# Rotation tables of a two-layer attention trunk: one pass per group for all blocks, and loads that repeat the rows

## The chip, the cores and the metric

The kernel runs on one core of a Trainium2 chip. The metric is the device time of one execution in microseconds (us). The engines of the core are named as the profile names them: PE (TensorE, matrix products), DVE (VectorE), ACT (ScalarE), POOL (GpSimd) and SP (SyncE, which here issues every DMA).

## What is computed

The reference is a trunk of two layers over a sequence of 2048 frames with 1024 channels. Each layer projects its input, runs four groups of attention heads side by side, gates them, projects the result back and applies a layer norm. Two of the four groups rotate queries and keys by position:

```
def _rope(x, positions):
    d = x.shape[-1]
    inv_freq = ROPE_THETA ** (-jnp.arange(0, d, 2) / d)
    ang = positions[..., None] * inv_freq
    cos, sin = jnp.cos(ang)[:, :, None, :], jnp.sin(ang)[:, :, None, :]
    x1, x2 = jnp.split(x, 2, axis=-1)
    return jnp.concatenate([x1 * cos - x2 * sin, x2 * cos + x1 * sin], axis=-1)

def _layer(x, ...):
    proj = x @ w_in                       # 14 parts
    ya = banded attention with relative bias     (A: own chunk + 8 before)
    yb = latent attention; q_rope and k_rope of 32 channels are rotated   (B)
    yc = banded attention; q and k of 64 channels are rotated             (C: own chunk + 2 before)
    ym = attention to 256 memory tokens                                   (M)
    y = concat(ya*silu(ag), yb*silu(bg), yc*silu(cg), ym*silu(mg)) @ w_out
    return layer_norm(alpha * x + y)
```

The angles depend on the positions alone, not on the layer.

## The kernel before

The sequence is cut into four blocks of 512 frames (`BT`), and everything is held with channels on the 128 partitions and frames along the row. Products keep fp32 accuracy by splitting each operand into a high and a low part (`xh`, `xl`, `whi`, `wlo`) and adding three products.

For each layer the program lists units: for each block one unit of C for each pair of heads, M, A, C, M, A (24 units), then for each pair of heads and block a unit of B (`unit_b`, 8 units). A unit has a fill (projections, rotation, row maxima: small steps) and attention banks. `drive` puts the fill of the next unit between the banks of the present one. `later(dt, f)` puts work some modelled time behind. The framework then orders the instructions of each engine by its own estimate; each engine executes its queue in order, and all DMAs go out on SP's queue in order.

Rotation tables: group 0 (C) has 32 frequencies, group 1 (B) has 16. A table has 128 rows: for a block, row p holds the cosine (or the sine with a sign) of position x frequency p mod 32 (or mod 16). `trig(b, gs)` loads the 512 positions of block b, repeated over 128 partitions (L281), converts them (L283, DVE), and for each group runs 11 more DVE instructions and two sines on ACT, whose function tables are switched to the sine and back to the exponential, and stores the tables in DRAM (L300, L301). It is called in layer 0 alone: group 0 of block 0 in `mem_kv` at the start, group 1 of block 0 in the first M unit, and both groups of block b + 1 in the last A unit of block b.

The tables come back through two buffers `cts` (cosine, sine; one of each, 256 KB), at three places: L731 and L732 in each unit of C (group 0, 16 times in all), L827 and L828 in `latent` with k = 0 (group 1, 8 times), and L968 and L969 in `unit_b` (group 1, 16 times). In layer norm (`phase3`) `cts` holds the gain.

In `unit_b`, `qrdone` multiplies the projected rotary queries by the tables and, some modelled 3 us later, issues four loads that put them into the query tiles (L1035, L1036, named Y<-xh and Y<-xl). The products for the row maxima (`mx`) read them. The `tmp` tiles (5 buffers of 512 columns) hold the positions and the angles as well as loaded inputs and other short-lived values.

Of the kernel before, what the change touches and what calls it, by code (L numbers as in the profile page):

```python
# [149 lines left out]
def hybrid(ctx, tc, x, mem, positions, w_in, rel_bias, q_norm, w_uq, kv_norm, w_ukv,  # L150
# [17 lines left out]
    def act(out, a, fn, **kw):  # L168
        ck.use("act", 0.17 + 0.00083 * cols(out), out, a)
        return nc.scalar.activation(out, a, fn, **kw)  # L170
# [35 lines left out]
    def tmp(name, dt=F32):  # L206
        return sb.tile([128, BT], dt, name=name, tag="tmp", bufs=5)

    def rowcast(src, off, n):
        return bass.AP(tensor=src.tensor, offset=src.offset + off, ap=[[0, 128], [1, n]])  # L210
# [54 lines left out]
            return [o, o + 1024, o + 2048]  # L265
        return [4096 + 1024 * (b - 1), 4096 + 3072 + 1024 * (b - 1), 4096 + 6144 + 1536 * (b - 1)]

    cosT, sinT, memkv = {}, {}, {}
    h_src = [x[0, t * 128:(t + 1) * 128, :] for t in range(S // 128)]

    def setup_rows():
# [4 lines left out]
            act(rr[0:32, 0:c1 - c0], rf[0:32, 0:c1 - c0], AF.Copy)  # L276
            dma(f32(rowt)[:, c0:c1], f32(rr)[0:32, 0:c1 - c0])

    def trig(b, gs=(0, 1)):
        pi = tmp("pi", I32)  # L280
        dma(pi, rowcast(positions, b * BT, BT))  # L281
        pf = tmp("pf")
        nc.vector.tensor_copy(pf, pi)  # L283
        for g in gs:
            ang, kk = tmp("ang"), tmp("kk")
            nc.vector.tensor_scalar(ang, pf, rc[:, g:g + 1], None, op0=OP.mult)
            nc.vector.tensor_scalar(kk, ang, float(np.float32(1.0 / TWO_PI)), ROUND, op0=OP.mult, op1=OP.add)
            nc.vector.tensor_scalar(kk, kk, -ROUND, None, op0=OP.add)
            for pc in (PC1, PC2, PC3):
                stt(ang, kk, -pc, ang, op0=OP.mult, op1=OP.add)  # L290
            nc.vector.tensor_scalar(ang, ang, 3.1415925, -3.1415925, op0=OP.min, op1=OP.max)
            nc.vector.tensor_scalar(kk, ang, -1.0, None, op0=OP.mult)
            tt(kk, kk, ang, op=OP.max)
            nc.vector.tensor_scalar(kk, kk, -1.0, float(np.float32(math.pi / 2)), op0=OP.mult, op1=OP.add)
            act(ang, ang, AF.Sin)
            act(kk, kk, AF.Sin)
            nc.vector.tensor_scalar(ang, ang, rc[:, 2 + g:3 + g], None, op0=OP.mult)
            cosT[g, b] = dram.tile([128, BT], F32, name=f"cos{g}{b}")
            sinT[g, b] = dram.tile([128, BT], F32, name=f"sin{g}{b}")
            dma(cosT[g, b], kk)  # L300
            dma(sinT[g, b], ang)  # L301


    wsrc = []
# [420 lines left out]
    def unit_c(l, b, p, D):  # L725
        qq = [next_q(), next_q()]
        st = {}
        fill = []

        def tabl():  # L730
            dma(cts[0], cosT[0, b])  # L731
            dma(cts[1], sinT[0, b])  # L732
            if p == 0 and b:
                for k in range(2):
                    dma(f32(Kc[k][0])[:, 0:128], f32(Kc[k][0])[:, BT:BT + 128])
                    dma(f32(Kc[k][1])[0:64, 0:128], f32(Kc[k][1])[0:64, BT:BT + 128])
                dma(f32(Vc)[:, 0], f32(Vc)[:, 4])
        fill.append((0.0, tabl))

        def kdone(r):  # L740
            for k in range(2):
                split_k(r[k], Kc[k][0][:, 128:], Kc[k][1][:, 128:])

        def qdone(r):
            for i in range(2):
                split_q(r[i], 0.125, *qq[i])
            st["q"] = True

        def gdone(pg):
            st["ge"] = gate_tiles(pg)  # L750

        def maxes(i):
            h = 2 * p + i
            k1 = Kc[p][0]
            q1, q2 = qq[i]

            def one(t):
                def f():
                    if t == 0:
                        ck.until(lambda: "q" in st)  # L760
                        st["mc", i] = mcol(4)
                    mc = st["mc", i]
                    if t % 2 == 0:
                        st["m"] = bank("mx", "mx")
                    lo = 0 if b or t else 128
                    o = 256 * (t % 2)
                    mt = st["m"][:, o + lo:o + 256]
                    ck.tick(mmc(mt, q1[:, 128 * t:128 * t + 128], k1[:, 128 * t + lo:128 * t + 256], True, True))
                    ttr(mt, cmask[:, lo:256], mc[:, t:t + 1], snk[:, 4 * l + h:4 * l + h + 1])
                    if t == 3:  # L770
                        max_row(mc, q2, 64, st, i)
                return f
            return [(0.107, one(t)) for t in range(4)]

        pq = project((l, b, 10 + 2 * p), lambda pp: rope(pp, qdone))
        pg = project((l, b, 11 + 2 * p), gdone)
        if p == 0:
            fill += project((l, b, 8), lambda pp: rope(pp, kdone))
            fill += pq
            fill += project((l, b, 9), lambda pp: put_v(pp, Vc, 1, 4))  # L780
            fill += pg
            late = maxes(0) + maxes(1)
        else:
            fill += pq
            lat = []
            for k in range(3):
                lat += project((l, b, 18 + k), lambda pp, k=k: latent(l, b, k, pp, D))
            fill += lat + [(0.0, lambda: latent_fin(l, b, D))]
            fill += pg
            late = maxes(0) + maxes(1)  # L790
        if p == 0:
            fill = fill[:-4] + mix(fill[-4:], late)
        else:
            fill = fill[:-8] + mix(fill[-8:], late)
        banks = []
        for i in range(2):
            h = 2 * p + i
            q1, q2 = qq[i]
            k1, k2 = Kc[p]
            hd = mk_head(st, i, 64 * p, lambda: st["ge"], D["gT"][4 + p, b], srow[p])  # L800

            def sink(q2=q2, h=h):
                bias = snk[64:65, 4 * l + h:4 * l + h + 1]
                act(es[0:1], f32(q2)[64:65], AF.Exp, bias=bias)
                ef = tmp("ef")
                act(ef[0:1], f32(q2)[64:65], AF.Exp, bias=bias)
                tt(es[32:33], ef[0:1], f32(es)[0:1], op=OP.subtract)

            def sg(t, q0, qe, col):
                ks = slice(128 * t, 128 * t + 128)  # L810
                vh, vl = vst(Vc, t, p)
                return seg(q0, qe, col, d64_ops(k1[:, ks], k2[0:73, ks], q1, q2, q0, qe), vh, vl)
            bl = head_banks(hd, [[sg(1, 0, 256, 0), sg(2, 128, 384, 256)],
                                 [sg(3, 256, 512, 0), sg(4, 384, 512, 256)] + ([sg(0, 0, 128, 384)] if b else [])])
            bl[0]["sink"] = sink
            banks += bl
        return fill, banks

    def latent(l, b, k, p, D):
# [4 lines left out]
        if n == 64:  # L824
            nc.gpsimd.memset(sf[64:128], 0.0)
        if k == 0:
            dma(cts[0], cosT[1, b])  # L827
            dma(cts[1], sinT[1, b])  # L828
            D["sums", b] = sb.tile([128, 3, 4], F32, name="sums", bufs=2)
        later(0.8, lambda: dma(D["lat"][k, b][:n], cf[:n]))  # L830
        if k == 1:
# [117 lines left out]
    def unit_b(l, b, p, D):  # L949
# [13 lines left out]
        def loads():  # L963
            for k in (0, 2):
                dma(f32(lat[k]), f32(D["lathl"][k, b]).rearrange("p (s c) -> p s c", s=2))
            for z in range(2):
                dma(f32(lat[1])[64 * z:64 * z + 64, 0], f32(D["lathl"][1, b])[:, BT * z:BT * z + BT])
            dma(cts[0], cosT[1, b])  # L968
            dma(cts[1], sinT[1, b])  # L969
            for i in range(2):  # L970
                kh, kl = kpart(i, b)
                dma(f32(kh)[96:101], f32(rowt)[26:31, 0:BT])
                dma(f32(kh)[64:96], f32(D["kr"][0, b]))
                dma(f32(kl)[64:96], f32(D["kr"][1, b]))
            if (b, p) in ((0, 0), (1, 0)):
                for q in qq:
                    dma(f32(q[0])[97:101, :], f32(rowt)[4:8, 0:BT])
            v = vpart(b)
            nc.gpsimd.memset(f32(v)[:, :, 1, :], 1.0)
            nc.gpsimd.memset(f32(v)[:, :, 4, :], 0.0)  # L980
            for i in range(2):
                g = sb.tile([128, BT], F32, name="gm", tag="gate", bufs=6)
                st["ge", i] = g
            dma(st["ge", 0], D["gB"][p, b])
            later(2.5, lambda: act(st["ge", 1], st["ge", 0], AF.Exp, scale=-1.0))
# [207 lines left out]
    def mem_kv(kq):  # L1193
# [2 lines left out]
        wload(0)  # L1196
        f()
        dma(rc, rope_c)
        trig(0, (0,))
        wload(1)  # L1200
        run_fill(st)
        wsplit(0)
# [215 lines left out]
    for l in range(L):  # L1418
# [13 lines left out]
        else:  # L1432
            kq()
            load_mem(l)
        units = []
        for b in range(NB):
            us = [unit_c(l, b, 0, D), None, None, None, None, None]
            us[1] = unit_m(l, b, 0, D)
# [9 lines left out]
            if b == 0:  # L1448
                us[2] = ([(0.0, lambda: (ka(), bias_tables(l, D)))] + us[2][0], us[2][1])
            if l == 0 and b == 0:  # L1450
                us[1][0].insert(0, (0.0, lambda: trig(0, (1,))))
            if l == 0 and b + 1 < NB:
                us[5][0].insert(2, (0.0, lambda b=b: trig(b + 1)))
            units += us
        for p in range(2):
            for b in range(NB):
# [62 lines left out]
```

## Time and profile before

| | |
|---|---|
| time, 3 runs | 2660.25 us median, 2650.18 to 2664.6 |
| the profiled execution's own time | 2660.33 us |
| its span, first to last instruction | 2658.5 us |
| mean granted TensorE clock | 0.984 |
| busy | PE 2517.0 us (95%), DVE 1864.5 (70%), ACT 1258.8 (47%), POOL 1071.2 (40%) |
| DMA | 350.90 MB in 176443 packets, mean 132 GB/s |

Busy shares are averages over the span; an idle stretch of PE is what costs time. The granted clock is the share of full speed at which PE was allowed to run.

### The profile page before, as it was taken

The numbers are of one execution on the slowest core, as the hardware profiler recorded it, in microseconds if no ns is written. First come the engines' busy times: TensorE is split into PE (matmuls) and PEld (weight loads), VectorE is DVE, ScalarE is ACT, GpSimd is POOL, SyncE is SP. The second block draws the span as 40 slices with busy tenths as digits, with TensorE's granted clock in tenths as the row PEclk, the third lists the DMA queues.
The fourth block names the chain that finished last, engine by engine and source line by source line (L and its number), as shares of the span: only waits on it lengthen the run. The fifth ranks groups of instructions, "written<-read, shape, count | busy, mean of one in ns | idle before, by whom it ended". The sixth has DMA issues, their size and how long they took to land. (4 is left out here: it accounts for less than half of the span.)

```text
span 2658.5 us, 36518 instructions
## 1 busy us (share of the span) xinstructions
PE 2517.0 (95%) x12312; PEld 2072.1 (78%) x12312; DVE 1864.5 (70%) x3309; ACT 1258.8 (47%) x2251; POOL 1071.2 (40%) x835
## 2 busy tenths in 40 slices
PE   7999999999999899989999999999999999999998
PEld 6777877877888777768877778788788777777786
DVE  4667767658666877878766566567567577588786
ACT  4544455545544566650025444454454555666200
POOL 3343434343443344353343434434434433435343
PEclk9999999999999999999999999999999999999999
DMA  6555345345345423244445443443443453232432
GB/s 208 159 159 168 107 140 158 110 132 166 106 129 169 150 78 98 71 152 145 140 136 160 150 145 127 126 138 118 143 139 115 144 168 104 68 114 78 150 124 87
DMA packets 176443, 350.90 MB, mean 132 GB/s; under 512 B 25689, under 2 KB 48945, under 8 KB 176257
## 3 DMA queue, kind: packets, MB, share of 16 engines
q1 hardware_dynamic: 176256, 348.58, 41.9%
q8 instruction: 98, 1.61, 0.3%
q14 instruction: 89, 0.72, 0.1%
HBM read 247.43 MB, written 68.02 MB: 119 GB/s over the span
## 5 line engine op out<-in xcount | busy, mean ns | idle before, releaser
L182 POOL TENSOR_TENSOR wlo<-raw,whi 128x1024 fp32r<-128x1024 f32 (+1 forms) x192 | 459.5, 2393 | 660.5 <-ACT whi L170 622.9
L350 PE MATMUL pp<-xh,whi 128*128 128x512 f32 x1472 | 591.8, 402 | 7.0 <-DVE Y L174 4.4
L350 PE MATMUL pp<-xl,whi 128*128 128x512 f32 x1472 | 583.4, 396 | 4.6 <-DVE xl L174 4.5
L350 PE MATMUL pp<-xh,wlo 128*128 128x512 f32 x1472 | 580.1, 394 | 0.0
L170 ACT ACTIVATE ph<-sc 128x512 fp32r<-128x512 f32 (+2 forms) x560 | 324.1, 579 | 359.5 <-PE sc L350 350.5
L350 PE MATMUL sc<-Y 96*128 96x512 f32 (+16 forms) x1840 | 454.8, 350 | 11.8 <-DMA Y<-mr 5.8
L174 DVE TENSOR_TENSOR pl<-p,ph 128x512 fp32r<-128x512 f32 (+2 forms) x389 | 319.6, 823 | 186.9 <-ACT p L170 182.2
L350 PE MATMUL pv<-ph,Y 128*128 128x512 f32 (+3 forms) x1520 | 396.7, 341 | 9.3 <-DVE e L178 5.4
L350 PEld LDWEIGHTS sc<-Y 96*128 96x128 f32 (+6 forms) x1840 | 315.9, 193 | 56.0 <-DMA Y<-mr 5.7
L170 ACT ACTIVATE whi<-raw 128x1024 fp32r<-128x1024 f32 x192 | 203.6, 1060 | 325.2 <-PE pp L350 119.2
L182 POOL TENSOR_TENSOR pl<-p,ph 128x512 fp32r<-128x512 f32 (+1 forms) x171 | 221.1, 1293 | 329.0 <-ACT p L170 243.5
L350 PEld LDWEIGHTS pp<-xh,whi 128*128 128x128 f32 x1472 | 279.6, 190 | 63.1 <-issue 5.1
L350 PEld LDWEIGHTS pp<-xh,wlo 128*128 128x128 f32 x1472 | 278.7, 189 | 59.2
L170 ACT ACTIVATE p<-sc 128x512 f32<-128x512 f32 (+2 forms) x560 | 322.4, 576 | 0.8 <-DVE pl L174 0.4
L350 PEld LDWEIGHTS pp<-xl,whi 128*128 128x128 f32 x1472 | 279.9, 190 | 49.8 <-DVE xl L174 6.7
L350 PEld LDWEIGHTS pv<-ph,Y 128*128 128x128 f32 x1520 | 271.3, 191 | 50.1 <-issue 5.9
L350 PE MATMUL pv<-pl,Y 128*128 128x512 f32 (+3 forms) x760 | 265.0, 349 | 34.3 <-DVE pl L174 22.4
L350 PE MATMUL mx<-Y 128*128 128x256 f32 (+6 forms) x800 | 249.6, 339 | 23.7 <-DVE Y L178 10.9
L495 DVE CUSTOM_DVE_ANT_0 mx<-mx,bts 128x128 f32<-128x128 f32 (+3 forms) x352 | 171.9, 495 | 73.3 <-PE mx L350 66.7
L350 PEld LDWEIGHTS mx<-Y 128*128 128x128 f32 (+1 forms) x800 | 148.4, 191 | 77.8 <-DVE Y L178 17.7
L182 POOL TENSOR_TENSOR g<-g,e 128x128 f32<-128x128 f32 x192 | 116.6, 616 | 206.3 <-DVE e L190 191.6
L350 PEld LDWEIGHTS pv<-pl,Y 128*128 128x128 f32 x760 | 145.4, 191 | 65.6 <-DVE pl L174 33.5
(235 smaller groups left out, 3594.4 us busy)
## 6 DMA issues: line engine op xcount, KB each, us to landing
raw<-in_w_in_dram SPq DMA_DIRECT2D x184, 512.0 KB
Y<-Y SPq DMA_DIRECT2D x144, 128.0 KB
gr<-gT SPq DMA_DIRECT2D x64, 256.0 KB
gT<-g SPq DMA_DIRECT2D x48, 256.0 KB
cts<-sin SPq DMA_DIRECT2D x40, 256.0 KB
cts<-cos SPq DMA_DIRECT2D x40, 256.0 KB
xt<-in_xT_dram SPq DMA_DIRECT2D x32, 256.0 KB
raw<-in_w_out_dram SPq DMA_DIRECT2D x16, 512.0 KB
```

What stands on the lines that cost most here:

```text
L170: return nc.scalar.activation(out, a, fn, **kw)
L174: return nc.vector.tensor_tensor(out, a, b, **kw)
L182: return nc.gpsimd.tensor_tensor(out, a, b, **kw)
L350: mm(o, lhs, rhs, start=start, stop=stop)
L495: nc.vector.tensor_tensor_reduce(m, m, table, op0=OP.add, op1=OP.max, scale=1.0, scalar=floor, accum_out=acc)
```

## The change

One pass per group makes the tables of all four blocks: block b has its positions on partitions 32b to 32b + 31 (four loads of 32 partitions, `trig_pos`), so that row 32b + i is block b's frequency i. The pass is a list of 13 steps (`trig`): group 0 runs at the start as before, group 1 is mixed step by step into the fill of the first M unit. The passes for blocks 1 to 3 are gone. Each group stores three parts in one DRAM tile: cosine, and sine and its negative in the order that the group needs; the sign is no longer a multiplication by a constant column.

The loads (`tload`) now repeat rows: the cosine load reads the 32 rows of a block four times; the sine table is put together from pieces that alternate between sine and negative sine, two loads of 64 partitions for group 0, four of 32 partitions for group 1.

```
-    def trig(b, gs=(0, 1)):
+    def trig_pos():
         pi = tmp("pi", I32)
-        dma(pi, rowcast(positions, b * BT, BT))
-        pf = tmp("pf")
-        nc.vector.tensor_copy(pf, pi)
-        for g in gs:
-            ang, kk = tmp("ang"), tmp("kk")
...
-            act(ang, ang, AF.Sin)
-            act(kk, kk, AF.Sin)
-            nc.vector.tensor_scalar(ang, ang, rc[:, 2 + g:3 + g], None, op0=OP.mult)
-            cosT[g, b] = dram.tile([128, BT], F32, name=f"cos{g}{b}")
-            sinT[g, b] = dram.tile([128, BT], F32, name=f"sin{g}{b}")
-            dma(cosT[g, b], kk)
-            dma(sinT[g, b], ang)
+        for b in range(NB):
+            dma(pi[32 * b:32 * b + 32], bass.AP(tensor=positions.tensor, offset=positions.offset + b * BT,
+                                                ap=[[0, 32], [1, BT]]))
+        return pi
+
+    def trig(g, pi):
...
+        def start():
+            st["a"], st["k"] = tmp("ang"), tmp("kk")
+            nc.vector.tensor_copy(st["k"], pi)
+        def sine():
+            act(st["a"], st["a"], AF.Sin)
+            act(st["k"], st["k"], AF.Sin)
+            t = trigt[g] = dram.tile([3 * 128, BT], F32, name=f"trig{g}")
+            dma(t[0:128], st["k"])
+            dma(t[128 * (1 + g):128 * (2 + g)], st["a"])
+        def neg():
+            st["n"] = tmp("nsin")
+            nc.vector.tensor_scalar(st["n"], st["a"], -1.0, None, op0=OP.mult)
+            dma(trigt[g][128 * (2 - g):128 * (3 - g)], st["n"])
...
+
+    def tload(g, b):
+        t = trigt[g][32 * b:32 * b + 1, 0:1]
+        n = 32 >> g
+        dma(cts[0], bass.AP(tensor=t.tensor, offset=t.offset, ap=[[0, 4], [BT, 32], [1, BT]]))
+        for i in range(2 + 2 * g):
+            r = slice(2 * n * i, 2 * n * i + 2 * n)
+            dma(cts[1][r], bass.AP(tensor=t.tensor, offset=t.offset + 128 * BT,
+                                   ap=[[(128 + g * n) * BT, 2], [BT, n], [1, BT]]))
...
         def tabl():
-            dma(cts[0], cosT[0, b])
-            dma(cts[1], sinT[0, b])
+            tload(0, b)
...
-            dma(cts[0], cosT[1, b])
-            dma(cts[1], sinT[1, b])
+            tload(1, b)
...
-            dma(cts[0], cosT[1, b])
-            dma(cts[1], sinT[1, b])
+            tload(1, b)
...
-        trig(0, (0,))
+        for f_ in trig(0, trig_pos()):
+            f_()
...
             if l == 0 and b == 0:
-                us[1][0].insert(0, (0.0, lambda: trig(0, (1,))))
-            if l == 0 and b + 1 < NB:
-                us[5][0].insert(2, (0.0, lambda b=b: trig(b + 1)))
+                us[1] = (mix(us[1][0], [(0.0, lambda: tg.extend(trig(1, trig_pos())))]
+                             + [(0.0, lambda: tg.pop(0)())] * 13),) + us[1][1:]
```

## Rows read from the trace of the kernel before

**Rows 1.** Head of the page and busy time by engine.
```profile
span 2658.5 us, 36518 instructions
...
PE 2517.0 (95%) x12312; PEld 2072.1 (78%) x12312; DVE 1864.5 (70%) x3309; ACT 1258.8 (47%) x2251; POOL 1071.2 (40%) x835
```
**Rows 2.** Windows, L827 of block 0 to 3, layers 0 and 1 (columns in its heading).
```profile
core 0: us, PE busy (x) PEld busy (x) DVE busy (x) ACT busy (x) POOL busy (x), PEclk, DMA share, GB/s
147.50:758.10 610.60, 582.67 (x2920) 483.49 (x2919) 427.94 (x785) 307.91 (x520) 243.17 (x166) 0.98 0.44 137
1450.00:2049.10 599.10, 585.11 (x3017) 485.04 (x3016) 381.78 (x716) 292.51 (x502) 240.44 (x166) 1.00 0.42 133
```
**Rows 3.** Groups of PE, 1450 to 2049.1 us: busy, mean ns, idle before.
```profile
L393 PE MATMUL px<-identr,xt 128*128 128x128 f32 x96 | 14.1, 273 | 0.7 <-DMA xt<-h 0.7
```
**Rows 4.** Timeline of PE: start, duration, instruction, [idle before, and what ended it].
```profile
216.16 1.19 PE L350 MATMUL pv<-ph,Y 128*128 128x512 f32 x2 [5.36 <-DVE e L178]
...
599.79 0.80 PE L350 MATMUL mx<-Y 128*128 128x256 f32 x2 [3.72 <-DVE Y L178]
```
**Rows 5.** Windows round the first and the third pass, columns as in rows 2.
```profile
205.00:225.00 20.00, 14.64 (x66) 11.94 (x65) 19.66 (x34) 11.71 (x17) 4.15 (x4) 0.83 0.47 151
...
590.00:640.00 50.00, 43.69 (x204) 36.61 (x203) 38.51 (x64) 23.95 (x38) 16.54 (x11) 0.90 0.50 156
```
**Rows 6.** List of DMA issues, 84 groups: first, two others, last.
```profile
raw<-in_w_in_dram SPq DMA_DIRECT2D x184, 512.0 KB
...
cts<-sin SPq DMA_DIRECT2D x40, 256.0 KB
...
Y<-mr SPq DMA_DIRECT2D x128, 2.0 KB
...
rowt<-rr SPq DMA_DIRECT2D x1, 16.0 KB
```
**Rows 7.** Packets and SP's queue on the page: packets, MB, share of 16 engines.
```profile
DMA packets 176443, 350.90 MB, mean 132 GB/s; under 512 B 25689, under 2 KB 48945, under 8 KB 176257
...
q1 hardware_dynamic: 176256, 348.58, 41.9%
```
**Rows 8.** Timelines of SP and PE in a unit_b of layer 0.
```profile
909.94 0.33 SPq L968 DMA_DIRECT2D cts<-cos  x1
910.66 0.33 SPq L969 DMA_DIRECT2D cts<-sin  x1
...
912.67 0.58 SPq L1035 DMA_DIRECT2D Y<-xh  x1
...
916.45 0.62 PE L350 MATMUL mx<-Y 96*128 96x512 f32 x2
```
**Rows 9.** Timelines of SP and PE in a unit_b of layer 1.
```profile
2324.23 0.34 SPq L968 DMA_DIRECT2D cts<-cos  x1
...
2325.43 0.39 SPq L969 DMA_DIRECT2D cts<-sin  x1
2326.99 1.21 SPq L1035 DMA_DIRECT2D Y<-xh  x2
...
2329.08 0.47 PE L350 MATMUL mx<-Y 96*128 96x512 f32 x1 [0.22 <-DMA Y<-xh]
```
**Rows 10.** Timelines of SP and DVE at the start of layer 1.
```profile
1369.00 0.34 SPq L732 DMA_DIRECT2D cts<-sin  x1
...
1371.85 0.69 DVE L174 TENSOR_TENSOR u<-pp,cts 128x512 f32<-128x512 f32 x1 [1.18 <-DMA cts<-sin]
```
**Rows 11.** Windows over the B units of both layers, columns as in rows 2.
```profile
860.00:1180.00 320.00, 294.16 (x1393) 237.99 (x1391) 254.36 (x456) 210.49 (x411) 141.12 (x119) 0.98 0.34 106
2150.00:2410.00 260.00, 243.59 (x1171) 198.43 (x1170) 200.41 (x395) 164.40 (x326) 101.16 (x92) 0.97 0.35 105
```
**Rows 12.** Waits of PE: us in all, times, longest.
```profile
PE mx L350 <- DMA Y<-xh: 0.5, 2, 0.2
```

More of the change, by code (lines that the diff above doesn't have):

```diff
@@ L266, in mla_kv @@
         return [4096 + 1024 * (b - 1), 4096 + 3072 + 1024 * (b - 1), 4096 + 6144 + 1536 * (b - 1)]
-    cosT, sinT, memkv = {}, {}, {}
+    trigt, memkv = {}, {}
     h_src = [x[0, t * 128:(t + 1) * 128, :] for t in range(S // 128)]
@@ L277, in setup_rows @@
             dma(f32(rowt)[:, c0:c1], f32(rr)[0:32, 0:c1 - c0])
-    def trig(b, gs=(0, 1)):
+    def trig_pos():
         pi = tmp("pi", I32)
-        dma(pi, rowcast(positions, b * BT, BT))
-        pf = tmp("pf")
-        nc.vector.tensor_copy(pf, pi)
-        for g in gs:
-            ang, kk = tmp("ang"), tmp("kk")
[L286 to L294, printed above, removed]
-            act(ang, ang, AF.Sin)
-            act(kk, kk, AF.Sin)
-            nc.vector.tensor_scalar(ang, ang, rc[:, 2 + g:3 + g], None, op0=OP.mult)
-            cosT[g, b] = dram.tile([128, BT], F32, name=f"cos{g}{b}")
-            sinT[g, b] = dram.tile([128, BT], F32, name=f"sin{g}{b}")
-            dma(cosT[g, b], kk)
-            dma(sinT[g, b], ang)
@@ new lines, in trig_pos, with sc, red @@
+        for b in range(NB):
[3 more added lines that the diff above has]
+    def trig(g, pi):
+        st = {}
+        def sc(o, i, *c, **k):
+            return lambda: nc.vector.tensor_scalar(st[o], st[i], *c, **k)
+        def red(pc):
+            return lambda: stt(st["a"], st["k"], -pc, st["a"], op0=OP.mult, op1=OP.add)
+        def start():
[11 more added lines that the diff above has]
+            dma(trigt[g][128 * (2 - g):128 * (3 - g)], st["n"])
+        return [start,
+                sc("a", "k", rc[:, g:g + 1], None, op0=OP.mult),
+                sc("k", "a", float(np.float32(1.0 / TWO_PI)), ROUND, op0=OP.mult, op1=OP.add),
+                sc("k", "k", -ROUND, None, op0=OP.add)] + [red(pc) for pc in (PC1, PC2, PC3)] + [
+                sc("a", "a", 3.1415925, -3.1415925, op0=OP.min, op1=OP.max),
+                sc("k", "a", -1.0, None, op0=OP.mult),
+                lambda: tt(st["k"], st["k"], st["a"], op=OP.max),
+                sc("k", "k", -1.0, float(np.float32(math.pi / 2)), op0=OP.mult, op1=OP.add),
+                sine, neg]
@@ L1435, in hybrid @@
         units = []
+        tg = []
         for b in range(NB):
```

## Prediction

> **What bounds the kernel now.** The head of the page comes first: TensorE (PE) is busy for 95% of a span of 2658.5 us [rows 1], so whatever leaves PE alone is worth nothing, and whatever stops PE counts in full. I then looked for a stretch that does the same work with and without the table passes. Layer 1 makes no tables, so I cut both layers at the same instruction, the first table load of the q latent (L827), from block 0 to block 3, and asked for busy times by stretch [rows 2]. Layer 0 needs 610.6 us, layer 1 599.1 us. The counts show that the comparison is clean: DVE has 785 - 716 = 69 more instructions in layer 0 and ACT 520 - 502 = 18 more, which is what the passes for blocks 1 to 3 issue there (6 groups of 11 and 3 casts on DVE; 12 sines and 6 loads of ACT's tables). PE has 97 more in layer 1, 96 of them the transposes by which layer 1 gets its input, 14.1 us busy [rows 3]. Next I asked PE's timeline for the waits inside those passes. PE stands still for 5.36 us for DVE e, and 3.72 us for DVE Y; three more such gaps (2.25, 3.29, 2.52 us) lie at 388, 397 and 627 us [rows 4]: DVE executes in order, and the table arithmetic, or its wait for the positions, stands ahead of what PE needs. After each gap the granted clock falls: 0.83 of full speed over 20 us round the first pass, 0.90 over 50 us round the third, against 1.00 in layer 1's whole stretch [rows 2, 5]. Last, I read the DMA part of the page, the list of DMA issues and SP's timeline where the tables are loaded, since that is where the change adds work.
>
> **What the passes give back.** Blocks 1 to 3 lose their passes: 69 DVE instructions, 427.94 - 381.78 = 46.2 us of DVE, and 15.4 us of ACT [rows 2]. Most of that runs under PE and is worth nothing. What PE gets back I bound from both sides. Below: 610.6 - 599.1 = 11.5 us, as if the transposes cost nothing. Above: 11.5 + 14.1 = 25.6 us, as if each transpose held PE for its whole duration. A second way: PE idles 27.9 us in layer 0 and 14.0 in layer 1, 13.9 more, and 2% of the clock over 610.6 us is another 12.2; together 26.1, partly the same time twice, since idle time at a low clock counts in both. I take 20.
>
> **What stays.** The start still has one pass of about the same 12 DVE instructions and 2 sines; its positions come by four loads instead of one, three more issues of some 0.35 us on SP ahead of the weight and input loads, but one temporary buffer fewer is held. The pass for the second group is the same work, now spread over one unit. Its start instruction has to wait for the last of four position loads, and the wait stands at the head of DVE's queue with the q splits and row maxima behind it, for which PE waits. For both I take nothing, with -4 to +4 as ends. Ten table stores go away (16 to 6).
>
> **The loads that repeat rows.** This is the added work. 80 loads of 256 KB become 168: per table pair one of 256 KB, and two of 128 KB (first group, 16 times) or four of 64 KB (second group, 24 times). Three things count.
>
> First, SP: 88 more issues at about 0.35 us [rows 8, 9], 31 us of a queue that in most places waits for others soon after. Alone it makes what stands behind a load late by 0.4 to 1.1 us.
>
> Second, the engines that carry them. The bytes are the same, but not the shape: the DRAM side of the cosine load begins with a count of 4 (four copies), and that of each sine piece with a count of 2. How many of the 16 DMA engines a load of few rows uses can be counted. The list has 1,695 issues in 84 groups [rows 6]. If every issue ended with one small packet on each of 16 engines, that would be 27,120 packets; with the 896 that carry rows of 4, 16 or 32 bytes (gn, rc and snk) 28,016 packets below 512 B. The page counts 25,689 [rows 7], 2,327 fewer. 212 issues in the list move 4, 5, 8 or 9 rows (128 of them are the Y<-mr loads of 4 rows [rows 6]); if each uses as many engines as it has rows, 2,328 packets are missing. So a load of few rows runs on few engines. In all of these the outermost count is also the number of rows, so the rows don't say which of the two decides for a load of 128 rows that begins with a count of 4.
>
> By outermost count, the cosine load runs on 4 engines, 64 KB each, and all sine pieces on 2, together 128 KB each. If these are the same lowest engines, the busiest two get 192 KB per table pair instead of 32 KB. The queue moved 348.58 MB in 41.9% of 16 engines' span [rows 7]: 348.58 MB / (0.419 x 16 x 2658.5 us) = 19.6 KB per us and engine. So a table pair takes 192/19.6, about 10 us, instead of 1.7. By rows it stays at 1.7. Between these ends I take 10, because the only loads in this trace with a small outermost count run on that count. The Trainium skill states the rule outright (DMA: Bandwidth & Descriptors, "Rules for kernel authors"): the slowest dimension of the access patterns sets the number of engines, and a leading broadcast of c copies confines a DMA to at most c. By that rule the sum is the one below; by 16 engines it is the first rival's. The packet count agrees as far as it goes; no run so far shows the broadcast itself.
>
> Third, who waits. Not the reader of the table: in unit_b it is loaded one unit ahead. But everything on the same queue that is issued behind has a share on the two busy engines. In unit_b the order on SP is fixed by when cts comes free: the next unit's table pair is issued, and 2 us later the rotated queries of this unit (L1035). In one unit these are at 909.94, 910.66 and 912.67, and PE's first row-maximum product, which reads them, starts at 916.45 [rows 8]. In another the pair is at 2324.23 and 2325.43, the queries at 2326.99, and the product waits 0.22 us for them and starts at 2329.08 [rows 9]: 2.1 us from issue to use, no slack. With 10 us of work ahead on two engines, the queries land at about 909.9 + 10 + 1.4 = 921.3 and 2324.2 + 11.4 = 2335.6; PE stands still for 4.9 and 6.5 us. SP's timeline shows the queries within 4 us behind the sine load in 9 of the 16 units; in two of these the product comes some 20 us later, in seven within 0 to 4 us. Seven stalls of 2 to 6.5 us, at 4.5: 31 us. Then the clock: a gap of 5.36 us was followed by 0.17 x 20 = 3.4 us of lost clock [rows 4, 5]; at 2 us for each, 14. Finally the start of layer 1, where the table can't be loaded ahead because cts holds the layer norm's gain: DVE already waits 1.18 us for the sine load [rows 10]. 10 - 1.7 = 8.3 us more at most, with the second projection as cover; I take 7. Delayed weight loads and row-maximum rows (Y<-mr) I take at nothing, with 10 us as the upper end.
>
> **Sum.** 2660.3 us (the profiled execution's own time, 2658.5 of span and 1.8 round it; the median of the runs is the same to 0.1 us) - 20 + 31 + 14 + 7 = 2692 us. Ends: with stalls of 2 us each, no clock, 3 us in layer 1 and the full 25.6 back, 2660.3 - 25.6 + 14 + 3 = 2652; with 11.5 back, stalls of 6.5, 3.4 us of clock each, 8.3, and 10 for the rest, 2660.3 - 11.5 + 45.5 + 23.8 + 8.3 + 10 = 2736.
>
> **Rivals.** (1) Faster: the repeated loads use all 16 engines, or their delay stays below what the queries can bear. For it: the bytes are the same, and a cts pair lands long before its use nearly everywhere. Against it: the packet count. The point that decides is whether a pair still lands within about 4 us; then only SP's 0.4 to 1.1 us is left at seven places, and the time is 2660.3 - 20 = 2640. (2) A draw: few engines, but DVE, which is 77 to 79% busy in these stretches [rows 11] and makes PE wait elsewhere, uses the stall to catch up, and the pair runs faster alone than the mean rate; stalls of 2 to 3 us (17 in all) and 3 in layer 1 against 20 back give 2660. (3) The arithmetic pays nothing, because the units' ends in layer 0 have other late work: then PE's idle time there would not fall to layer 1's, and with a hidden load the time stays at 2660; layer 1's counts speak against it [rows 2].
>
> **How the numbers follow.** What this kernel's measurement can tell from no change is about 0.5%, 13 us: faster is below 2647, slower above 2673. Few engines with PE stopped: 0.62, slower. Rivals 2 and 3 together 0.18, no change. Rival 1 0.20, faster. The likeliest case's own range is 2652 to 2736; the stated range must take in rival 1 as well, since cases of both signs hold weight: 2638 to 2732.
>
> **What would show it.** The packets below 512 B tell the engines directly: 1,776 issues are to be expected, and with 4 and 2 engines 25,689 - 1,280 + 416 + 48 - 160 = 24,713 packets, with 16 engines 26,985. The gain: the stretch of layer 0 shrinks from 610.6 to some 590 us, DVE's count there to 716, the clock to 1.00. The loss: PE's waits for DMA Y<-xh, 0.5 us in all before [rows 12], grow to some 30 us, in seven units of both layers, with half-clock after them; DVE waits up to 8 us for cts at the start of layer 1. The prediction is wrong if PE doesn't wait for DMA Y<-xh although the packets show few engines (the queries bear more than I think), or if the packets show 16.

## Result and the profile after

The changed kernel takes 2698.93 us (median of 4 runs, 2690.86 to 2700.69); the kernel before took 2658.3 us in the same session (4 runs, 2650.18 to 2664.6). The ratio is 1.0148, 95% interval 1.0121 to 1.0174: slower by 1.5%. The profiled execution of the changed kernel took 2690.86 us, its span is 2689.1 us. It is the fastest of the four: the medians differ by 40.6 us, the spans of the two profiled executions by 30.6, so some 10 us of the loss stand in none of the stretches below. One run of a later experiment (only the cosines cut) took 4050.61 us at a granted clock of 0.555 and is left out of its time. The head of the page of the changed kernel, its packets and SP's queue, to be read against [rows 1, 7]:

```profile
span 2689.1 us, 36492 instructions
...
PE 2520.9 (94%) x12312; PEld 2073.8 (77%) x12312; DVE 1822.3 (68%) x3240; ACT 1243.3 (46%) x2233; POOL 1069.7 (40%) x835
...
DMA packets 173803, 347.50 MB, mean 129 GB/s; under 512 B 24712, under 2 KB 47968, under 8 KB 173616
...
q1 hardware_dynamic: 173616, 345.17, 41.3%
```

DVE lost 69 instructions and ACT 18, as counted. Packets below 512 B: 24,712. The prediction gave 24,713 for loads on 4 and 2 engines and 26,985 for 16, so the repeating loads run on few engines. The Trainium skill has it as a rule (DMA: Bandwidth & Descriptors, "Rules for kernel authors") that a leading broadcast of c copies confines a DMA to at most c engines. This count agrees with it.

Where did 30.6 us of span come from? PE executes 12,312 instructions in both kernels, so I cut both spans where PE has executed the same number of them (the x of PE, which agree to one in each stretch). Windows of the changed kernel, the columns as in [rows 2]: start, layer 0's blocks 0 to 3, unit_b, start of layer 1, its blocks 0 to 3, unit_b. The two stretches that are left out are 169.1 and 158.5 us long, against 169.0 and 158.5.

```profile
0.00:157.60 157.60, 119.13 (x598) 100.16 (x599) 85.70 (x161) 72.41 (x124) 54.07 (x55) 0.90 0.55 169
157.60:746.60 589.00, 574.74 (x2920) 474.82 (x2919) 386.70 (x715) 292.04 (x502) 244.44 (x166) 1.00 0.44 136
746.60:1204.20 457.60, 416.36 (x1980) 339.27 (x1979) 327.07 (x595) 261.97 (x498) 188.35 (x160) 0.97 0.39 117
...
1373.30:1467.10 93.80, 81.11 (x377) 64.48 (x375) 51.50 (x96) 38.88 (x71) 31.83 (x18) 0.96 0.49 143
1467.10:2067.00 599.90, 584.44 (x3016) 484.89 (x3015) 382.35 (x716) 292.30 (x502) 240.75 (x166) 1.00 0.43 133
2067.00:2530.60 463.60, 429.03 (x2021) 349.23 (x2020) 337.79 (x608) 260.70 (x496) 188.64 (x163) 0.96 0.37 116
```

The kernel before in the four of these stretches that [rows 2] don't have:

```profile
0.00:147.50 147.50, 121.57 (x599) 101.17 (x600) 86.94 (x161) 71.96 (x124) 53.84 (x55) 0.94 0.59 177
...
758.10:1200.00 441.90, 413.00 (x1980) 336.56 (x1979) 330.48 (x599) 262.56 (x498) 191.70 (x162) 0.98 0.40 123
...
1369.00:1450.00 81.00, 78.13 (x377) 63.13 (x376) 54.42 (x96) 39.28 (x71) 31.98 (x18) 1.00 0.54 166
...
2049.10:2500.00 450.90, 420.75 (x2021) 341.93 (x2020) 334.52 (x607) 259.60 (x496) 191.06 (x163) 0.98 0.39 119
```

A stretch's length less PE's busy time is its idle time. A change of the busy time at the same count goes with the granted clock (PEclk, the third number from the end) in every stretch but the start, where the busy time falls by 2.4 us although the clock falls too, from 0.94 to 0.90; why is not shown. So each difference splits in two:

| stretch | before | after | difference | of it PE idle | of it PE busy |
|---|---|---|---|---|---|
| start | 147.5 | 157.6 | +10.1 | +12.5 | -2.4 |
| layer 0, blocks 0 to 3 | 610.6 | 589.0 | -21.6 | -13.7 | -7.9 |
| unit_b, layer 0 | 441.9 | 457.6 | +15.7 | +12.3 | +3.4 |
| start of layer 1 | 81.0 | 93.8 | +12.8 | +9.8 | +3.0 |
| layer 1, blocks 0 to 3 | 599.1 | 599.9 | +0.8 | +1.5 | -0.7 |
| unit_b, layer 1 | 450.9 | 463.6 | +12.7 | +4.4 | +8.3 |

There are three losses and one gain: the passes gave back 21.6 us, and the start, unit_b (28.4 in both layers) and the start of layer 1 lost 51.3 us.

**unit_b.** PE's waits over the whole span of the changed kernel (us in total, times, longest); before, Y<-xh was 0.5 us [rows 12] and Y<-mr the line in the second fence:

```profile
PE sc L378 <- DMA Y<-mr: 18.1, 8, 4.6
...
PE mx L378 <- DMA Y<-xh: 6.0, 4, 2.1
```

```profile
PE sc L350 <- DMA Y<-mr: 5.8, 6, 2.8
```

In unit_b alone the two waits together grew from 5.8 to 19.2 us; the rest of Y<-mr lies in the start and in the blocks. PE's wait for DVE Y grew in unit_b as well, from 1.8 to 8.6 us, but it is 7.6 us there with the loads cut (second experiment), so it does not come from the shape of the loads.

Y<-mr is the move of a finished row maximum into the query tile (4 rows of 128, L516), which the score product reads. One such place, timelines of SP and PE; compare [rows 8]:

```profile
883.10 0.60 SPq L325 DMA_DIRECT2D cts<-trig  x1
884.15 0.65 SPq L516 DMA_DIRECT2D Y<-mr  x1
886.34 1.22 SPq L1060 DMA_DIRECT2D Y<-xh  x2
...
888.28 1.35 SPq L328 DMA_DIRECT2D cts<-trig  x2
...
889.70 3.14 PE L378 MATMUL sc<-Y 101*128 101x512 f32 x9 [4.57 <-DMA Y<-mr]
```

The row maximum is issued 1.05 us behind the cosine load and is used 5.55 us later, with PE idle for 4.57 us of it.

**Start of layer 1.** DVE's timeline, against 1.18 us of wait for the sine load in [rows 10]:

```profile
1382.86 0.69 DVE L174 TENSOR_TENSOR u<-pp,cts 128x512 f32<-128x512 f32 x1 [7.92 <-DMA cts<-trig]
1385.65 0.69 DVE L174 TENSOR_TENSOR t<-pp,cts 128x512 f32<-128x512 f32 x1 [2.10 <-DMA cts<-trig]
...
1394.95 0.82 DVE L174 TENSOR_TENSOR t<-t,us 64x512 f32<-64x512 f32 x1 [2.39 <-DMA us<-u]
```

DVE waits 7.92 us for the table, then 2.39 us for a transfer that was queued behind the next table load.

**The start.** Timelines of SP and PE:

```profile
26.50 0.41 SPq L311 DMA_DIRECT2D trig<-nsin  x1
26.96 2.22 SPq L438 DMA_DIRECT2D xt<-in_mem_dram  x4
...
30.10 1.04 PE L378 MATMUL pp<-Y,whi 128*128 128x256 f32 x3 [15.96 <-ACT Y L170]
```

The last four loads of `mem` go out right behind the store of the negated sine, at 26.96 us, and PE stands still for 15.96 us until they are split. In the kernel before, three of them went out at 13.04 us and the fourth at 19.51.

### The profile page after: what moved, and what is told of

It reads as the page before. It is cut to its first block, busy times and chain, and to the rows that moved or that the text cites. A ratio compares the mean times of both kernels' runs of the same rounds, so it can differ in the third digit from the quotient of the medians.

```text
span 2689.1 us, 36492 instructions
## 1 busy us (share of the span) xinstructions
PE 2520.9 (94%) x12312; PEld 2073.8 (77%) x12312; DVE 1822.3 (68%) x3240; ACT 1243.3 (46%) x2233; POOL 1069.7 (40%) x835
## 2 busy tenths in 40 slices
DMA packets 173803, 347.50 MB, mean 129 GB/s; under 512 B 24712, under 2 KB 47968, under 8 KB 173616
## 3 DMA queue, kind: packets, MB, share of 16 engines
q1 hardware_dynamic: 173616, 345.17, 41.3%
## 5 line engine op out<-in xcount | busy, mean ns | idle before, releaser
L378 PE MATMUL sc<-Y 96*128 96x512 f32 (+16 forms) x1840 | 461.3, 354 | 28.0 <-DMA Y<-mr 18.1
```

What stands on the lines that cost most here:

```text
L378: mm(o, lhs, rhs, start=start, stop=stop)
```

## Experiments

All times are medians, taken in one session with the kernel before (2658 to 2661 us); ratios are to that kernel. "Cut" and "repeating" speak of the shape of the table loads.

### The buffer of the negated sine

```
         def neg():
-            st["n"] = tmp("nsin")
+            st["n"] = sb.tile([128, BT], F32, name="nsin", tag="p", bufs=PB)
```

> The changed kernel with one edit: the negated sine (nsin) gets a buffer of another set, the three in which probabilities are kept later, instead of one of the five temporary buffers that the loads of mem use too. Theory: the start is 10.4 us later than before (first load of the q latent's table at 157.9 instead of 147.5 us) because the last four mem loads are given their buffers behind nsin and so go out only at 26.96 us, behind the stores of the pass. Then the four go out at 13 to 20 us again, PE's gap of 15.96 us at 30.10 shrinks to a few us, the first table load comes at 148 to 150 us and the kernel takes about 2689 us. Rival: the start is late because of the four position loads and the third table store on SP's queue; then nothing moves and it stays at 2699 us.

Measured: 2695.83 us, ratio 1.0129 (1.0111 to 1.0147). Timelines of SP and PE:

```profile
13.81 2.96 SPq L438 DMA_DIRECT2D xt<-in_mem_dram  x3
...
26.16 0.32 SPq L305 DMA_DIRECT2D trig<-kk  x1
...
82.04 1.16 SPq L328 DMA_DIRECT2D cts<-trig  x2
83.31 0.54 SPq L325 DMA_DIRECT2D cts<-trig  x1
...
86.87 1.36 SPq L516 DMA_DIRECT2D Y<-mr  x2
...
95.74 1.51 PE L378 MATMUL sc<-Y 73*128 73x256 f32 x6 [6.17 <-DMA pi<-in_positions_dram]
```

The mechanism is as the theory had it: three mem loads go out at 13.81 us again, PE's gap shrinks from 15.96 to 5.17 us, and PE has executed 193 instructions at 52.2 us (50.0 before, 61.0 in the changed kernel). The time is not: at 367 instructions PE is at 103.5 us (89.9 before, 101.8 in the changed kernel), since a score product waits 6.17 us on the way. Its row maxima were issued 3 us behind a repeating table pair. The trace puts the wait down to the position loads behind them on the queue, which landed last, so that alone does not say whose fault it was; the sixth run does. The rival, that nothing would move at the start, is refuted.

### The loads cut at their copies

```
-        dma(cts[0], bass.AP(tensor=t.tensor, offset=t.offset, ap=[[0, 4], [BT, 32], [1, BT]]))
-        for i in range(2 + 2 * g):
...
+        for i in range(4):
+            dma(cts[0][32 * i:32 * i + 32], bass.AP(tensor=t.tensor, offset=t.offset, ap=[[BT, 32], [1, BT]]))
+        for i in range(4 + 4 * g):
+            dma(cts[1][n * i:n * i + n], bass.AP(tensor=t.tensor, offset=t.offset + (128 + (i % 2) * (128 + g * n)) * BT,
+                                                 ap=[[BT, n], [1, BT]]))
```

> The changed kernel with every repeating load cut at its copies: four loads of 32 rows for the cosines, four of 32 rows (first group) or eight of 16 rows (second group) for the sines, 8 or 12 issues per table pair instead of 3 or 5. Bytes and contents are the same. Theory of few engines: with 16 packets for each load there are 24,712 - 416 + 6,656 = 30,952 packets below 512 B, the load is off PE's path again, unit_b's two stretches go from 626.5 and 622.1 us back to about 611 and 609, the start of layer 1 from 93.8 to about 81, and the kernel takes 2699 - 41 = 2658 us, plus up to 12 us for the queue, which gets 248 more issues. Rival, the price is that of the issues on SP: the same places lose more than in the changed kernel, and it takes 2710 us or more.

Measured: 2650.78 us, ratio 0.9965 (0.9952 to 0.9978), so faster than the kernel before. Packets on the page:

```profile
DMA packets 180045, 347.54 MB, mean 131 GB/s; under 512 B 30952, under 2 KB 54208, under 8 KB 179856
```

30,952 is the number that 16 engines for each load should give. PE's waits for the two moves, 24.1 us in the changed kernel:

```profile
PE sc L378 <- DMA Y<-mr: 2.0, 4, 0.8
...
PE mx L378 <- DMA Y<-xh: 0.9, 2, 0.6
```

By windows at the same PE counts, unit_b is 1.5 and 0.9 us longer than before in the two layers, the start of layer 1 2.4 us, and the passes' gain stays (591.3 us). In these stretches 248 more issues on SP cost at most these 4.8 us. The rival is refuted. The time is 7 us below the theory's 2658: the 41 us were read from an execution 8 us below its kernel's median, and the start is 4.5 us shorter as well (153.1 us).

### The kernel before with repeating loads

```
+    def tload(g, b):
+        t = cosT[g, b][0:1, 0:1]
+        dma(cts[0], bass.AP(tensor=t.tensor, offset=t.offset, ap=[[0, 4], [BT, 32], [1, BT]]))
+        t = sinT[g, b][0:1, 0:1]
+        n = 32 >> g
+        for i in range(2 + 2 * g):
+            dma(cts[1][2 * n * i:2 * n * i + 2 * n], bass.AP(tensor=t.tensor, offset=t.offset,
+                                                             ap=[[3 * n * BT, 2], [BT, n], [1, BT]]))
...
-            dma(cts[0], cosT[1, b])
-            dma(cts[1], sinT[1, b])
+            tload(1, b)
```

> The kernel before with all its passes and its stored tables, and only the loads changed: the cosines as four copies of 32 rows, the sines in pieces of two blocks of rows, so that each access pattern begins with the same counts (4 and 2) as in the changed kernel, and there are as many issues. Theory: the loads alone cost what unit_b and the start of layer 1 lose: stretches of about 626 and 622 us in unit_b instead of 611 and 609, 94 instead of 81 us at the start of layer 1, no change in layer 0's first stretch (610.6) or at the start (147.5), in all 2658 + 41 = 2699 us. Rival: the losses come from the new order of the work that the passes leave behind; then this kernel stays at 2658 us.

Measured: 2717.83 us, ratio 1.0209 (1.0188 to 1.0230). unit_b loses 17.9 and 16.0 us, the start of layer 1 13.4, together 47.3 (41.2 in the changed kernel); the start loses 5.5 and the other blocks 4.3 and 2.2, which I had not expected, so the time is 19 us above the theory's 2699. With all passes in place the loads alone cost some 57 us: they are the whole loss and more. The rival is refuted.

### Rows repeated by the stores

```
+        def store(b):
+            def f():
+                ct = cosT[g, b] = dram.tile([128, BT], F32, name=f"cos{g}{b}")
+                sn = sinT[g, b] = dram.tile([128, BT], F32, name=f"sin{g}{b}")
+                r = slice(32 * b, 32 * b + 32)
+                for c in range(4):
+                    dma(ct[32 * c:32 * c + 32], st["k"][r])
+                for c in range(4):
+                    dma(sn[32 * c:32 * c + 32], st["n" if c % 2 and not g else "a"][r])
+            return f
...
+        dma(cts[0], cosT[g, b])
+        dma(cts[1], sinT[g, b])
```

> The changed kernel's one pass per group, but the rows are repeated by the stores instead of by the loads: for each block and group eight stores of 32 rows write the 128-row tables of the kernel before, and each load is one of 128 rows again, two per table pair; nsin has the buffer of the first experiment. 64 stores in place of 6, 80 loads in place of 168. Theory: the gain of the passes stays (589 us in layer 0's stretch), and the start (147.5 to 150 us), unit_b (611 and 609 us) and the start of layer 1 (81 us) go back to those of the kernel before: 2658 - 21 = 2637 us. Rival: 58 more stores, 20 us of SP's queue, nearly all of it in the first block, take the gain back: 2650 to 2660 us.

Measured: 2646.77 us, ratio 0.9949 (0.9933 to 0.9964). The passes' stretch is 588.7 us, unit_b 0.6 and 2.8 us shorter than before, the start of layer 1 0.2 longer: the theory holds there. But the start is 14.8 us longer than before (162.3 us), and the time is 10 us above the theory's 2637. The 64 stores are issued in that stretch, the first group's spread over it by `later`. That they are the reason, as the rival says, is likely and not shown apart from the rest; what is lost there is some two thirds of the gain, not all of it.

### Loads alone

A small program that only loads, one kind after the other; a DVE add reads each tile, and nothing else is on the queue.

> A small kernel that computes nothing of the model: it only makes loads, one kind after the other, four times over, with nothing else on the queue. A VectorE add reads each loaded tile, so that the time from SP's issue to the add is the load's. Alone: cosines of 128 rows (256 KB), cosines as four copies of 32 rows (256 KB), sine pieces of 2 x 32 rows (128 KB) and of 2 x 16 rows (64 KB), and four query moves of 32 rows from SBUF to SBUF (64 KB each) as in unit_b. Then table pairs with the four query moves issued behind: 128-row loads; the changed kernel's loads of the first and of the second group; the same cut at the copies. Theory of few engines: the repeating cosines take about 64 KB / 19.6 KB per us = 3.3 us of transfer where the 128-row load takes 0.8, and the query moves behind the changed kernel's pairs land up to 8 us later than behind the 128-row pair; behind the cut pairs they land like behind the 128-row pair. Rival, all shapes use all engines: all land alike, to 0.5 us.

Timelines of DVE and SP, second round; the idle time in brackets is close to the time from SP's issue to the landing, since DVE has nothing else to do. In order: cosines of 128 rows; as four copies; four query moves alone; the moves behind a pair of 128-row loads, behind a first-group pair, and behind a second-group pair, with the first issue of that pair.

```profile
102.40 0.17 DVE L176 TENSOR_TENSOR end<-end,cos 128x8 f32<-128x8 f32 x1 [2.52 <-DMA cos<-tab]
...
108.16 0.17 DVE L176 TENSOR_TENSOR end<-end,cos 128x8 f32<-128x8 f32 x1 [4.97 <-DMA cos<-tab]
...
123.58 0.17 DVE L176 TENSOR_TENSOR end<-end,probe 128x8 f32<-128x8 f32 x1 [4.00 <-DMA probe<-q]
...
130.22 0.17 DVE L176 TENSOR_TENSOR end<-end,probe 128x8 f32<-128x8 f32 x1 [4.00 <-DMA probe<-q]
...
143.54 0.17 DVE L176 TENSOR_TENSOR end<-end,probe 128x8 f32<-128x8 f32 x1 [8.96 <-DMA probe<-q]
...
144.94 0.60 SPq L195 DMA_DIRECT2D cos<-tab  x1
...
156.29 0.17 DVE L176 TENSOR_TENSOR end<-end,probe 128x8 f32<-128x8 f32 x1 [7.01 <-DMA probe<-q]
```

Four copies take 4.97 us instead of 2.52 for the same 256 KB. On 4 engines each carries 64 KB instead of 16; 48 KB more in 2.45 us is 19.6 KB per us and engine, the rate worked out from the page before; the third and the fourth round, with 2.17 and 2.85 us more, give 22 and 17. The moves wait 5.0 and 3.0 us longer behind repeating pairs, less than the 8 at the upper end. In part that is because in this program they are issued 3.0 and 4.4 us behind the pair's first issue rather than 2; the other 2 to 3 us are not explained. Behind the cut first-group pair they took 3.90 us, but there they were issued 3.1 us after the last load, so that case does not tell much. The rival is refuted.

### Both repairs together

The cut loads and the buffer of the first experiment (both diffs above).

> The second experiment's cut loads together with the first one's buffer for nsin. Theory: two causes added up at the start. The buffer makes the mem loads late and costs 11 us until 50 us of the span, and a narrow table load at 80 us, ahead of the row maxima, cost 8 us in the first experiment. With both gone TensorE starts its 598th instruction at about 148 to 150 us (157.6 in the changed kernel, 156.5 with the buffer alone, 153.1 with the cut loads alone), and the kernel takes 2650.8 - 4 = about 2646 us. Rival: four position loads and a third table store cost the start as much; then the 598th instruction stays at 153 us and the time at 2651 us.

Measured: 2640.37 us, ratio 0.9921 (0.9901 to 0.9942): 0.8% faster than the kernel before and the best version here. The start takes 144.2 us, 3.3 less than before, and PE has executed 367 instructions at 90.2 us (89.9 before, 103.5 with the buffer alone). The first experiment's wait of 6.17 us is gone, and only the loads' shape differs between the two: it was the loads. The four versions side by side:

| | nsin from `tmp` | own buffer |
|---|---|---|
| repeating loads | 2698.9 | 2695.8 |
| cut loads | 2650.8 | 2640.4 |

The loads cost 48 to 55 us, the buffer 10 us once the loads no longer cover it.

### Only the cosines cut, only the sines cut

Each takes one half of the second experiment's diff.

> The changed kernel with only the cosine loads cut into four of 32 rows; the sine pieces stay on counts of 2. Packets below 512 B: 24,712 - 160 + 2,560 = 27,112. The two busiest engines then have 128 KB per table pair instead of 192: 128/19.6 = 6.5 us instead of 9.8. Theory, the delay of what is queued behind counts: about half of the 41 us in unit_b and at the start of layer 1 is left, in all 2670 to 2685 us. Rival, any load on few engines costs its full price, however long it takes: 2695 to 2700 us. Rival, the cosine load was the cause: 2655 us.

> The changed kernel with only the sine pieces cut, into four of 32 rows or eight of 16; the cosine load stays at a count of 4. Packets below 512 B: 24,712 - 256 + 4,096 = 28,552. The busiest engines then have 64 KB per pair: 3.3 us instead of 9.8. Theory: below about 4 us the queries and row maxima have slack, so unit_b loses 5 us or less in each layer and the start of layer 1 some 4 us: 2655 to 2665 us. Rival, a load on few engines costs its full price however long it takes: 2695 us. Rival, the sine pieces were harmless and the cosine load was the cause: 2690 us.

Measured: 2668.34 us (nine runs), ratio 1.0033 (1.0013 to 1.0053), with the cosines cut; 2663.82 us, ratio 1.0015 (1.0003 to 1.0028), with the sines cut. Packets below 512 B are 27,112 and 28,552, as expected. The table shows what unit_b and the start of layer 1 lose against the kernel before in the profiled executions; the two sums are unit_b of layer 0, start of layer 1, unit_b of layer 1. The kilobytes per table pair are worked out as in the prediction: they assume that cosines and sines share the same lowest engines, and the trace does not name a packet's engine.

| version | KB on the busiest engine | loss, us |
|---|---|---|
| changed kernel; with own buffer; kernel before with its loads | 192 | 41.2; 47.9; 47.3 |
| cosines cut | 128 + 16 | 6.9 + 9.0 + 9.9 = 25.8 |
| sines cut | 64 + 16 | 4.2 + 2.9 + 11.5 = 18.6 |
| all cut; with own buffer | 32 | 4.8; 4.1 |
| rows repeated by the stores | 32 | -3.2 |

Both pieces cost something, and both rivals (full price for any such load; one piece harmless) are refuted: by the medians the kernel is 17.6 us slower than with all loads cut when only the cosines are cut, and 13.0 us when only the sines are. Which piece costs more is less clear. The last column falls with the kilobytes, but unit_b alone loses nearly the same in both, 16.8 and 15.7 us, and PE waits longer for Y<-mr and Y<-xh with the sines cut (10.6 and 8.1 us) than with the cosines cut (8.7 and 0.7).

With the cosines cut the time is just below the theory's 2670 to 2685 us. With the sines cut it lies in the theory's range, but the theory's point, hardly any harm below 4 us, is not borne out: the busiest engines need 80/19.6 = 4.1 us per pair, at that point, and 13.0 us are still lost. The 11.5 us of unit_b in layer 1 come from a profiled execution that is the slowest of ten (2671.27 us).

### Another queue

```
-    def tload(g, b):
+    def tload(g, b, dma=dma):
...
-            tload(1, b)
+            tload(1, b, nc.scalar.dma_start)
```

The last two lines stand in `unit_b`.

> The changed kernel with the table loads of unit_b alone issued by ScalarE instead of SyncE, so that they go through another queue; shapes, engines and bytes are the same, and everything else stays on SyncE's queue. Theory, what counts is the place in one queue: the queries and row maxima are no longer behind the table pair and land as before, PE's waits for Y<-mr and Y<-xh fall from 24.1 to below 8 us, and unit_b's stretches lose 28 us less, 2671 us, but for what 64 more issues cost ScalarE (64 + 16 at some 0.5 us, up to 10 us where its work is late). Rival, the engines are the limit whichever queue a transfer comes from: the queries wait as long as in the changed kernel, 2699 us or more.

Measured: 2733.92 us, ratio 1.0271 (1.0249 to 1.0292). PE's waits:

```profile
PE sc L378 <- DMA Y<-mr: 19.5, 10, 6.1
...
PE pp L378 <- ACT p L170: 17.4, 4, 6.8
...
PE mx L378 <- DMA Y<-xh: 12.3, 5, 5.4
```

The waits for the two moves don't fall to 8 us, they rise from 24.1 to 31.8, and PE waits 17.4 us for ACT's probabilities (3.3 in the changed kernel). The forecast of the queue theory, 2671 us, is missed by far. How much of the loss belongs to ACT, whose own work stands behind the issues, this run doesn't say, so the tenth takes the model away:

> Again a small kernel that only makes loads and computes nothing of the model. Three kinds of table pair (two loads of 128 rows; the changed kernel's loads of the first and of the second group), each issued once by SyncE and once by ScalarE, which has nothing else to do; behind each, on SyncE's queue, come either four query moves of 32 rows or one move of 4 rows of 128 like that of the row maxima. Read is the time from the first query move's issue to the VectorE add that reads it. In the fifth run it was 4.0 us behind the 128-row pair, 9.1 and 7.0 us behind the repeating pairs of the first and second group. Theory after the ninth run, the engines are the limit: with the pair on the other queue the moves are still 2 us or more later than behind the 128-row pair, and a move of 4 rows is late in the same way. Rival, the place in the queue is the limit and the ninth run lost its time by ScalarE's own issues: with the pair on the other queue the moves land after 4.0 us whatever its shape.

DVE's timeline in that program. The first five are the 4-row move behind a pair of 128-row loads issued by SP, then behind a first-group pair issued by SP and by ACT, and a second-group pair issued by SP and by ACT. The last five are the query moves behind a 128-row pair issued by SP, a first-group pair issued by SP and by ACT, and a second-group pair issued by SP and by ACT. Behind a 128-row pair issued by ACT it is 1.69 and 3.94 us.

```profile
78.67 0.17 DVE L176 TENSOR_TENSOR end<-end,probe 128x8 f32<-128x8 f32 x1 [1.75 <-DMA probe<-q]
...
96.00 0.17 DVE L176 TENSOR_TENSOR end<-end,probe 128x8 f32<-128x8 f32 x1 [7.85 <-DMA probe<-q]
...
105.64 0.17 DVE L176 TENSOR_TENSOR end<-end,probe 128x8 f32<-128x8 f32 x1 [5.27 <-DMA probe<-q]
...
119.37 0.17 DVE L176 TENSOR_TENSOR end<-end,probe 128x8 f32<-128x8 f32 x1 [6.31 <-DMA probe<-q]
...
130.49 0.17 DVE L176 TENSOR_TENSOR end<-end,probe 128x8 f32<-128x8 f32 x1 [5.37 <-DMA probe<-q]
138.01 0.17 DVE L176 TENSOR_TENSOR end<-end,probe 128x8 f32<-128x8 f32 x1 [3.97 <-DMA probe<-q]
...
158.66 0.17 DVE L176 TENSOR_TENSOR end<-end,probe 128x8 f32<-128x8 f32 x1 [8.90 <-DMA probe<-q]
...
170.31 0.17 DVE L176 TENSOR_TENSOR end<-end,probe 128x8 f32<-128x8 f32 x1 [7.30 <-DMA probe<-q]
...
183.65 0.17 DVE L176 TENSOR_TENSOR end<-end,probe 128x8 f32<-128x8 f32 x1 [6.82 <-DMA probe<-q]
...
196.37 0.17 DVE L176 TENSOR_TENSOR end<-end,probe 128x8 f32<-128x8 f32 x1 [6.97 <-DMA probe<-q]
```

A 4-row move lands after 1.7 us behind a wide pair and after 6.3 to 7.9 us behind a repeating one; from the other queue it still takes 5.3 to 5.4. The query moves gain 1.6 us of 4.9 by the other queue behind a first-group pair, and nothing behind a second-group pair. So most of the delay stays when the two transfers no longer share a queue, which fits the engines that both use. The Trainium skill says so as a rule (DMA: Bandwidth & Descriptors, "Issuing engines are not separate DMA queues"): transfers started by different engines run on the same 16 DMA engines. The runs agree, but for the up to 2.6 us that the other queue saved here.

## Why the prediction was right, and where its terms were not

The forecast was 2692 us, slower, with loads on few engines that stop PE. It came out at 2699 us, and undoing the loads alone takes 48 us away: direction and mechanism hold. That the number came so close is luck, as the sum below shows. Point by point:

- **What the passes give back** (20, between 11.5 and 26): 21.6 us, 18.5 to 23.0 in every version with the one pass. DVE's count is 715 (716 foreseen), the clock 1.00.
- **The engines and the rate**: packets 24,712 against 24,713. The pair's 10 us: the query moves behind a second-group pair landed 11.35 us after the pair's first issue when alone, against 10 + 1.4, and those behind a first-group pair after 11.92 us. No run shows the 1.4 us by itself.
- **Who waits** (seven stalls for Y<-xh, Y<-mr taken at nothing): this step failed. Y<-mr went from 5.8 to 18.1 us; Y<-xh, which was to grow to some 30 us in seven units, only from 0.5 to 6.0 in four places. I had followed the queries because they stood behind the pair in the trace before, though that trace already had PE wait 5.8 us for Y<-mr. The row maxima, moves of 4 rows, are delayed most when alone (from 1.75 to 7.85 us), and in the place shown above they stood behind the cosine load.
- **Stalls and clock in unit_b** (31 + 14 = 45): 28.4 us, of which 16.7 is PE idle and 11.7 a longer busy time, so the stalls were put twice too high and the clock about right.
- **Start of layer 1** (7): 12.8. DVE's wait was as foreseen, 7.92 us. That the transfers behind the next table load (`us`, and the weights, which I took at nothing) would come late too was not counted.
- **The start** (nothing, between -4 and +4): +10.1. "One temporary buffer fewer is held" was wrong: `nsin` is given out only after the sines, and the mem loads that share the set of buffers came out behind it. With a buffer of its own and cut loads the start is 3.3 us shorter than before.
- **The sum**: 32 us forecast, 30.6 in the span and 40.6 by the medians. It is that close because 17 us too much in unit_b stood against 16 too little at the two starts.
- **The first rival's point**, a pair landing within about 4 us, is not where it decides: at 4.1 us 13.0 us are still lost by the medians. How the loss grows from 32 to 192 KB is not settled: the medians are 2650.8, 2663.8, 2668.3 and 2698.9 us at 32, 80, 144 and 192 KB.

What stays open: which engines the repeating loads use, which no trace names; how much of the 60.6 us that unit_b lost in the run with ACT's queue (28.4 in the changed kernel) is ACT's own lateness; and why the second version still loses 2.4 us at the start of layer 1, where the table can't be loaded ahead.

## What to carry to other kernels

Before a DMA repeats rows, look at the count with which its access pattern begins: counts of 4 and 2 put the bytes on that many engines here, by the packet count, and what stood behind them waited, though the share of all 16 engines on the page was no higher than before (41.3%). Cutting the load at its copies cost 248 issues and won 48 us; count the small packets to see which case one has. And when a new temporary tile is given out late, ask which loads take their buffers from the same set.

## What the runs showed that was not expected

- SP's own issue of a repeating load is longer: 0.58 to 0.60 us for the cosines and 0.59 for a sine piece, against 0.32 to 0.38 us for a load of 128 rows and 0.42 for a cut one (medians in the two small programs). A second-group pair holds SP for about 3.2 us, where I had counted 1.75.
- 416 loads of 16 or 32 rows moved the same tables with 4.8 us of loss in unit_b and at the start of layer 1, where 168 repeating ones lost 41.
- A transfer of 2 KB in 4 rows was delayed more (6.1 us) than one of 256 KB in four moves of 32 rows (4.9 us), behind the same pair.
